# The output projection's low weight parts: negated on ScalarE and completed by an adding transfer

## The chip, the cores and the metric

The kernel runs on one core of one Trainium2 chip. The metric is the device time of one execution in microseconds (us); lower is better. A core has five engines that run side by side and wait for each other through semaphores: TensorE (PE in the rows, its weight loads PEld), VectorE (DVE), ScalarE (ACT), GpSimd (POOL) and SyncE (SP), and 16 DMA engines that carry out the transfers which SP, ACT and POOL issue.

## What is computed

One decoder layer on 256 tokens of width 2048. The reference, cut to what matters here:

```python
proj = jnp.einsum('bsd,de->bse', x, w_in[l])
q_mo, k_mo, v_mo, g_mo, u_gm, v_gm, g_gm, q_me, g_me = jnp.split(proj, IN_SPLIT_POINTS, axis=-1)
...
y_mo = moba_attention(q_mo, k_mo, v_mo).reshape(b, s, MOBA_W) * jax.nn.silu(g_mo)
y_gm = gmlp_spatial_gate(u_gm, v_gm, gmlp_ln_g[l], gmlp_ln_b[l], gmlp_w_s[l], gmlp_b_s[l]) * jax.nn.silu(g_gm)
...
y = jnp.concatenate([y_mo, y_gm, y_me], axis=-1)
sub = jnp.einsum('bse,ed->bsd', y, w_out[l])
x = layer_norm(DEEPNORM_ALPHA * x + sub, ln_g[l], ln_b[l])
```

The change concerns the last product, `y` (256 x 2048) by `w_out` (2048 x 2048), all in float32.

## The kernel before

Every large product is done with operands that are sums of two float32r parts, a high part `hi` and a low part `lo = w - hi`. Three matmuls, hi by hi, hi by lo and lo by hi, stand for one product (`mm3`, lines 105 to 107). So each weight that comes from memory is first split: ScalarE writes `hi` as a converted copy (line 100), VectorE writes `lo` as the raw weight minus `hi` (line 101).

The weights come as one stream of pieces of 128 x 1024 float32 (512 KB). The list STREAM gives their order; the last five items are the column blocks of `w_out`, three of 512 columns (8 pieces each) and two of 256 (4 pieces each): 32 pieces. `load_piece(n)` has a transfer issued on SP's queue into `wraw` (line 146) and the two split instructions. `wraw` has six buffers, `whi` and `wlo` four each (`bufs=LEAD + 1`). While piece n is multiplied, pieces up to n + 3 are asked for:

```python
for m in range(LEAD + 1):
    load_piece(first_piece[i] + j + m)
```

A buffer of `whi` or `wlo` can thus be written again once TensorE is through with the piece four places earlier; a buffer of `wraw` can be loaded again once its last reader is done. The tile framework puts in the waits and sets each engine's order; every engine and every queue works in its own order.

In the output projection a piece of a 512-wide item takes 12 matmuls of 512 columns: two tiles of rows, two halves of the tokens, three products. A piece of a 256-wide item has four tiles of rows and 24 matmuls of 256 columns. In the very last item (`apart=True`) the first half of the tokens goes through all four pieces, then the second half, so that the layer norm of the first half (`finish(0)`, lines 527 to 549, on DVE, ACT and POOL) lies beside the matmuls of the second. `finish(1)` ends the kernel.

Of the kernel before, what the change touches and what calls it, by code (L numbers as in the profile page):

```python
# [13 lines left out]
AF = mybir.ActivationFunctionType  # L14
ALU = mybir.AluOpType
# [16 lines left out]
MAGIC = 1.5 * 2.0 ** 23  # L32
PI_F = 3.1415925

# Column blocks of 128 of w_in: where each part of the projection starts.
Q_MO, K_MO, V_MO, G_MO, U_GM, V_GM, G_GM, Q_ME, G_ME = 0, 8, 16, 24, 32, 36, 40, 44, 48

# The weights' stream. ("T", matrix, block): 128 columns as the stationary operand, which gives the
# projection transposed; ("N", matrix, column, width): columns as the moving operand.
STREAM = [("N", "mem", 4 * P, NW)] + [("T", "mem", b) for b in range(4)]  # L40
STREAM += [("T", "in", Q_ME + b) for b in range(4)] + [("T", "in", G_ME + b) for b in range(4)]
for _g in range(2):
# [2 lines left out]
        STREAM += [("T", "in", K_MO + _h), ("T", "in", Q_MO + _h), ("T", "in", G_MO + _h)]  # L45
STREAM.append(("N", "in", V_GM * P, NW))
STREAM += [("T", "in", U_GM + b) for b in range(4)] + [("T", "in", G_GM + b) for b in range(4)]
# Rows of w_out in the order in which the mixed branches come to be ready.
OUT_ORDER = [0, 1, 2, 3, 4, 5, 6, 7, 12, 13, 14, 15, 8, 9, 10, 11]
OUT_COLS = [(0, 512), (512, 512), (1024, 512), (1536, 256), (1792, 256)]  # L50
STREAM += [("N", "out", c, w) for c, w in OUT_COLS]
# [1 line left out]
PIECE = 1024  # L53
# [2 lines left out]


def pieces_of(item):
    """How many pieces of PIECE elements per partition an item has, and the rows' tiles in each."""
    width = P if item[0] == "T" else item[3]  # L60
    kts = PIECE // width
    return KT // kts, kts, width
# [14 lines left out]
def hymba_layer(ctx: ExitStack, tc: tile.TileContext, xT, memT, x, pos, inv_freq, w, wsT, b_s,  # L77
                gln_g, gln_b, ln_g, ln_b, out):
    nc = tc.nc
# [9 lines left out]
    work = pool("work", 2)  # L89
# [3 lines left out]
    def f32(ap):  # L93
        return ap.bitcast(F32)
# [4 lines left out]
    def split(hi, lo, src):  # L99
        nc.scalar.activation(hi, src, AF.Copy)  # L100
        nc.vector.tensor_tensor(out=lo, in0=src, in1=f32(hi), op=ALU.subtract)  # L101

    def mm3(o, a, b, start, stop):
        """a.T @ b for operands that are exact sums of two float32r parts, (hi, lo)."""
        nc.tensor.matmul(o, a[0], b[0], start=start, stop=False)  # L105
        nc.tensor.matmul(o, a[0], b[1], start=False, stop=False)  # L106
        nc.tensor.matmul(o, a[1], b[0], start=False, stop=stop)  # L107

# [1 line left out]
    zero = const.tile([P, NW], BF16, name="zero")  # L110
    nc.vector.memset(zero, 0.0)
    idle = ps_side.tile([P, NW], F32, tag="side", name="idle")
    for _ in range(N_WARM):
        nc.tensor.matmul(idle, zero[:, :P], zero, start=True, stop=True)

# [1 line left out]
    pieces = []  # L117
    for i, item in enumerate(STREAM):
        n, kts, width = pieces_of(item)
# [8 lines left out]
    def load_piece(n):  # L128
        if n >= len(pieces) or n in ready:
            return  # L130
        i, j, kts, width = pieces[n]
        raw = wp.tile([P, kts, width], F32, tag="wraw", name="wraw", bufs=6)
        hi = wp.tile([P, kts, width], F32R, tag="whi", name="whi", bufs=LEAD + 1)
        lo = wp.tile([P, kts, width], F32R, tag="wlo", name="wlo", bufs=LEAD + 1)
        src = w[n].rearrange("p (k n) -> p k n", k=kts)
        if n == 0:
            a = wp.tile([P, S], F32, tag="araw", name="araw0", bufs=3)
            nc.sync.dma_start(a, memT[:, 0, :])
            for c in range(0, width, S):
                nc.sync.dma_start(raw[:, 0, c:c + S], src[:, 0, c:c + S])  # L140
            first.update(a=a, w=raw[:, 0, :])
            load_act(memT, memX, 1, 1)
            nc.sync.dma_start(raw[:, 1, :], src[:, 1, :])
            split(hi[:, 1, :], lo[:, 1, :], raw[:, 1, :])
        else:
            nc.sync.dma_start(raw, src)
            split(hi, lo, raw)
        if n == 1:
            split(memX[:, 0, 0, :], memX[:, 0, 1, :], first["a"])
        if 0 < n < first_piece[1]:  # L150
            load_act(memT, memX, kts * n, kts)
        ready[n] = (hi, lo)

# [1 line left out]
    memX = big.tile([P, KT, 2, S], F32R, tag="mem", name="memX")  # L155
    xX = big.tile([P, KT, 2, S], F32R, tag="x", name="xX")

# [2 lines left out]
        nc.sync.dma_start(raw[:, :n, :], src[:, k0:k0 + n, :])  # L160
        split(dst[:, k0:k0 + n, 0, :], dst[:, k0:k0 + n, 1, :], raw[:, :n, :])

# [1 line left out]
    slots, clock = {}, [0]  # L164

    def after(n, fn):
# [18 lines left out]
            yield j, kts, ready.pop(first_piece[i] + j)  # L185

    def proj_t(X, hook=None):
        """The next item's projection, transposed: [128 columns, 256 tokens], in SBUF."""
        assert STREAM[item[0]][0] == "T"
        acc = ps_acc.tile([P, 2, S], F32, tag="acc", name="acc")  # L190
        flat = acc.rearrange("p a s -> p (a s)")
        for j, kts, (hi, lo) in next_pieces(hook):
            for m in range(kts):
                k = j * kts + m
                nc.tensor.matmul(flat, hi[:, m, :], X[:, k].rearrange("p a s -> p (a s)"), start=k == 0, stop=False)  # L195
                nc.tensor.matmul(acc[:, 0, :], lo[:, m, :], X[:, k, 0, :], start=False, stop=k == KT - 1)  # L196
                if m % 4 == 3:
                    pump()
        part = work.tile([P, S], F32, tag="part", name="part")
        nc.scalar.activation(part, acc[:, 1, :], AF.Copy)  # L200
        r = work.tile([P, S], F32, tag="projT", name="projT")
        nc.vector.tensor_tensor(out=r, in0=acc[:, 0, :], in1=part, op=ALU.add)  # L202
        return r

    def proj_n(X, order=range(KT), hook=None, apart=False):
        """The next item's projection: two PSUM tiles of [128 tokens, columns]."""
        assert STREAM[item[0]][0] == "N"
        width = STREAM[item[0]][3]
        acc = [ps_acc.tile([P, width], F32, tag="acc", name="acc") for _ in range(NT)]

        def tile_of(t, j, kts, hi, lo):
            for m in range(kts):
                k = order[j * kts + m]
                tk = slice(t * P, (t + 1) * P)
                mm3(acc[t], (X[:, k, 0, tk], X[:, k, 1, tk]), (hi[:, m, :], lo[:, m, :]),
                    j + m == 0, j * kts + m == KT - 1)

        held = []
        for j, kts, (hi, lo) in next_pieces(hook):
            held.append((j, kts, hi, lo))  # L220
            if apart:
                tile_of(0, j, kts, hi, lo)
                continue
            for m in range(kts):
                k = order[j * kts + m]
                if X is memX and k == 0:
                    for c in range(0, width, S):
                        for t in range(NT):
                            nc.tensor.matmul(acc[t][:, c:c + S], first["a"][:, t * P:(t + 1) * P],
                                             first["w"][:, c:c + S], start=c == 0, stop=False)  # L230
                    continue
                for t in range(NT):
                    tk = slice(t * P, (t + 1) * P)
                    mm3(acc[t], (X[:, k, 0, tk], X[:, k, 1, tk]), (hi[:, m, :], lo[:, m, :]),
                        j + m == 0, j * kts + m == KT - 1)
                pump()
        if apart:
            yield acc[0]
            for h in held:
                tile_of(1, *h)  # L240
            yield acc[1]
        else:
            yield from acc

# [1 line left out]
    ident = const.tile([P, P], F32, name="ident")  # L246
    make_identity(nc, ident)
    causal = const.tile([P, 3, P], F32, name="causal")
# [2 lines left out]
        nc.gpsimd.affine_select(out=causal[:, b, :], in_=causal[:, b, :], compare_op=ALU.is_ge, fill=NEG / SCALE,  # L251
                                base=0, pattern=[[-1, P]], channel_multiplier=1)

# [1 line left out]
    cosT = const.tile([P, S], F32, name="cosT")  # L255
    sinT = const.tile([P, S], F32, name="sinT")

# [39 lines left out]
        nc.vector.tensor_scalar(out=sinT[P // 2:], in0=sinT[P // 2:], scalar1=-1.0, scalar2=None, op0=ALU.mult)  # L297

    def split_pair(src, tag, hi=0):
        """src as a tile with its two parts, the high one at index hi."""  # L300
        t = act.tile([P, 2, S], F32R, tag=tag, name=tag, bufs=4)
        split(t[:, hi, :], t[:, 1 - hi, :], src)
        return t
# [30 lines left out]
        nc.gpsimd.tensor_tensor(out=dst, in0=e[:, 0:1], in1=e[:, 1:2], op=ALU.pow)  # L334

    def values(acc, tag):
        """A projection in rows of tokens, as (hi, lo) by tile of tokens."""
        r = []
        for t in range(NT):
            v = act.tile([P, 2, NW], F32R, tag=tag, name=tag, bufs=2)  # L340
            split(v[:, 0, :], v[:, 1, :], acc[t])
            r.append(v)
        return r

# [1 line left out]
    def attention(q, k, v, h, gate, et, is_causal):  # L346
        wide = [P, 2 * P] if is_causal else [2 * P, 2 * P]
        at = [0, wide[0]]
# [68 lines left out]
        after(11, turn)  # L417
        after(14, weigh)

# [1 line left out]
    yX = [None]  # L421

    mv = values(list(proj_n(memX)), "mv")
# [12 lines left out]
        attention(qme[h], mk[h], mv, h, gme, 12 + h, False)  # L436
        gme[h] = silu2(proj_t(xX), "gme", 4)

# [1 line left out]
    late = {}  # L440

    def load_late():
# [23 lines left out]
        if grp == 0:  # L466
            load_late()

# [1 line left out]
    vl = []  # L470
    for acc in proj_n(xX):
        g = gelu2(acc, NW, act.tile([P, NW], F32, tag="vg", name="vg", bufs=2))
# [33 lines left out]
        nc.vector.scalar_tensor_tensor(out=y, in0=um[g], scalar=0.25, in1=gate, op0=ALU.mult, op1=ALU.mult)  # L506
        split(yX[0][:, 8 + g, 0, :], yX[0][:, 8 + g, 1, :], y)

# [1 line left out]
    xs, lg, lb = {}, {}, {}  # L510

    def load_x(n):
# [96 lines left out]
```

## Time and profile before

| | |
|---|---|
| Time of the two runs | 468.15 and 468.91 us, median 468.53 us |
| Span of the profiled execution | 466.4 us (the times count 2.1 us more, median against span) |
| TensorE busy | 449.5 us, 96% |
| VectorE busy | 343.5 us, 74% |
| ScalarE busy | 231.3 us, 50% |
| GpSimd busy | 14.4 us, 3% |
| Output projection's matmuls | from 365 to 453 us of the span |

The span is the time from the first to the last instruction of one profiled execution; no separate time of that execution is given beside it, so 468.53 - 466.4 = 2.1 us is taken for what lies around a span. Busy time is time in which an instruction of the engine was running; an engine can be busy a long time and bound nothing. In the profile L101 is line 101 of the kernel, and `wlo<-wraw,whi` an instruction that reads `wraw` and `whi` and writes `wlo`. A row of the timeline gives start, duration, engine, line, operation and, in brackets, how long the engine sat idle before it and what released it.

### The profile page before, as it was taken

What the parts mean: (1) busy time and instruction counts of PE and PEld (TensorE: products, weight loads), DVE (VectorE), ACT (ScalarE), POOL (GpSimd) and SP (SyncE); (2) the same over time, 40 slices, a digit from 0 to 9 for tenths busy, and PEclk for the clock granted to TensorE, in tenths of its full rate; (3) what the DMA queues carried; (4) which work ended last, traced back from release to release, by engine and by line L of the source; (5) the groups of instructions that cost most, each with busy time, mean ns of one, the idle gap of its engine ahead of it and who ended that gap; (6) DMA issues with size and microseconds to landing.
All of it is one profiled execution on the core that took longest, in us unless ns stands there. A gap on an engine that the chain in (4) does not pass through costs nothing.

```text
span 466.4 us, 6674 instructions
## 1 busy us (share of the span) xinstructions
PE 449.5 (96%) x2465; PEld 386.9 (83%) x2465; DVE 343.5 (74%) x582; ACT 231.3 (50%) x357; POOL 14.4 (3%) x23
## 2 busy tenths in 40 slices
PE   6999999999999999999999999999999999999980
PEld 3888888888888888888888888888888888888980
DVE  3879866776677988885778888858988746465666
ACT  4765754665444555554445545545655543334300
POOL 1000000000000000000000000000200000000033
PEclk9999999999999999999999999999999999999996
DMA  7998776545465555545655455876565557575123
GB/s 268 322 348 275 286 272 225 172 149 161 155 196 179 176 169 182 180 160 163 210 187 180 151 176 200 295 220 204 171 214 181 181 184 237 207 227 184 27 65 135
DMA packets 29552, 91.79 MB, mean 197 GB/s; under 512 B 3408, under 2 KB 5072, under 8 KB 29520
## 3 DMA queue, kind: packets, MB, share of 16 engines
q1 hardware_dynamic: 29232, 90.85, 58.9%
q10 hardware_dynamic: 288, 0.52, 0.3%
q8 instruction: 19, 0.31, 0.3%
q14 instruction: 13, 0.11, 0.1%
HBM read 89.26 MB, written 2.10 MB: 196 GB/s over the span
## 4 chain that ended last, share of the span: by engine, by line
PE 94%; DVE 3%; DMA 1%; SPq 0%; issue 0%; ACT 0%; DVEq 0%
PE acc L195 35%; PE acc L196 18%; PE acc L105 12%; PE acc L106 12%; PE acc L107 12%; DVE hX L544 2%; DMA wraw<-weights 1%; PE ptp L390 1%; DVE hX L545 1%; PE sc L105 1%; PE sc L106 0%; PE sc L107 0%; PE pv L107 0%; PE pv L105 0%; PE pv L106 0%
## 5 line engine op out<-in xcount | busy, mean ns | idle before, releaser
L101 DVE TENSOR_TENSOR wlo<-wraw,whi 128x1024 fp32r<-128x1024 f32 (+1 forms) x152 | 185.5, 1220 | 92.0 <-ACT whi L100 90.7
L100 ACT ACTIVATE whi<-wraw 128x1024 fp32r<-128x1024 f32 (+1 forms) x152 | 160.5, 1056 | 167.6 <-PE acc L195 61.8
L195 PE MATMUL acc<-xX,whi 128*128 128x512 f32 x640 | 227.4, 399 | 0.0
L196 PE MATMUL acc<-xX,wlo 128*128 128x256 f32 x640 | 179.4, 280 | 0.0
L195 PEld LDWEIGHTS acc<-xX,whi 128*128 128x128 f32 x640 | 120.2, 188 | 28.0
L196 PEld LDWEIGHTS acc<-xX,wlo 128*128 128x128 f32 x640 | 120.8, 189 | 0.1
L105 PE MATMUL acc<-whi,yX 128*128 128x512 f32 (+1 forms) x160 | 55.5, 347 | 0.0
L107 PE MATMUL acc<-whi,yX 128*128 128x512 f32 (+1 forms) x160 | 55.5, 347 | 0.0
L106 PE MATMUL acc<-wlo,yX 128*128 128x512 f32 (+1 forms) x160 | 55.5, 347 | 0.0
L105 PE MATMUL acc<-whi,xX 128*128 128x512 f32 x96 | 38.1, 397 | 0.0
L107 PE MATMUL acc<-whi,xX 128*128 128x512 f32 x96 | 37.5, 391 | 0.0
L106 PE MATMUL acc<-wlo,xX 128*128 128x512 f32 x96 | 37.4, 390 | 0.0
L105 PEld LDWEIGHTS acc<-whi,yX 128*128 128x128 f32 x160 | 30.3, 189 | 3.8
L107 PEld LDWEIGHTS acc<-whi,yX 128*128 128x128 f32 x160 | 30.3, 189 | 3.8
L106 PEld LDWEIGHTS acc<-wlo,yX 128*128 128x128 f32 x160 | 30.3, 189 | 3.7
L195 PE MATMUL acc<-memX,whi 128*128 128x512 f32 x64 | 22.6, 399 | 0.0
L107 PEld LDWEIGHTS acc<-whi,xX 128*128 128x128 f32 x96 | 18.0, 188 | 4.0
L105 PEld LDWEIGHTS acc<-whi,xX 128*128 128x128 f32 x96 | 18.0, 188 | 3.4
L106 PEld LDWEIGHTS acc<-wlo,xX 128*128 128x128 f32 x96 | 18.0, 188 | 3.3
L202 DVE TENSOR_TENSOR projT<-acc,part 128x256 f32<-128x256 f32 x44 | 18.1, 413 | 0.0
L196 PE MATMUL acc<-memX,wlo 128*128 128x256 f32 x64 | 18.0, 281 | 0.0
L200 ACT ACTIVATE part<-acc 128x256 f32<-128x256 f32 x44 | 16.1, 369 | 0.0
(147 smaller groups left out, 411.0 us busy)
## 6 DMA issues: line engine op xcount, KB each, us to landing
wraw<-weights SPq DMA_DIRECT2D x151, 512.0 KB, 3.5
araw<-xT SPq DMA_DIRECT2D x8, 256.0 KB, 4.5
araw<-memT SPq DMA_DIRECT2D x7, 256.0 KB, 5.8
xs<-xrow SPq DMA_DIRECT2D x6, 256.0 KB, 4.4
lnp<-ln_gv SPq DMA_DIRECT2D x4, 256.0 KB, 4.5
lnp<-ln_bv SPq DMA_DIRECT2D x4, 256.0 KB, 5.3
out<-hX SPq DMA_DIRECT2D x4, 256.0 KB, 2.6
xs<-xrow SPq DMA_DIRECT2D x4, 128.0 KB, 3.3
```

The source lines that it names most:

```text
L100: nc.scalar.activation(hi, src, AF.Copy)
L101: nc.vector.tensor_tensor(out=lo, in0=src, in1=f32(hi), op=ALU.subtract)
L105: nc.tensor.matmul(o, a[0], b[0], start=start, stop=False)
L106: nc.tensor.matmul(o, a[0], b[1], start=False, stop=False)
L107: nc.tensor.matmul(o, a[1], b[0], start=False, stop=stop)
L195: nc.tensor.matmul(flat, hi[:, m, :], X[:, k].rearrange("p a s -> p (a s)"), start=k == 0, stop=False)
L196: nc.tensor.matmul(acc[:, 0, :], lo[:, m, :], X[:, k, 0, :], start=False, stop=k == KT - 1)
L200: nc.scalar.activation(part, acc[:, 1, :], AF.Copy)
L202: nc.vector.tensor_tensor(out=r, in0=acc[:, 0, :], in1=part, op=ALU.add)
L390: nc.tensor.transpose(tp[:, n, :], st["p"][:, at[t] // P + b, :], ident)
L544: nc.vector.scalar_tensor_tensor(out=o, in0=o, scalar=mvr[:, 0:1], in1=g, op0=ALU.subtract, op1=ALU.mult)
L545: nc.vector.scalar_tensor_tensor(out=o, in0=o, scalar=rs, in1=b, op0=ALU.mult, op1=ALU.add)
```

## The change

For the pieces of `w_out` alone, `lo` is no longer written by VectorE. ScalarE writes `hi` as before and then minus `hi` into `lo`; GpSimd's queue issues a transfer from `wraw` to `lo`, both in SBUF, that adds what it carries to what stands there, `lo = -hi + w`. All other pieces keep their split. The rest of the diff takes comments out.

```diff
         else:
             nc.sync.dma_start(raw, src)
-            split(hi, lo, raw)
+            if STREAM[i][1] == "out":
+                nc.scalar.activation(hi, raw, AF.Copy)
+                nc.scalar.activation(lo, f32(hi), AF.Copy, scale=-1.0)
+                nc.gpsimd.dma_start(f32(lo), raw, accum_op=ALU.add)
+            else:
+                split(hi, lo, raw)
```

Lines move down by five behind this place: L146 is the same in both, L149 is the new activation and L150 the new transfer.

ScalarE at the seam between the last gate projections and the output projection, before (`th`, `part` and `yX` belong to the last mixed branch, the `whi` rows from here on to `w_out`):

```order
L316 ACTIVATE th<-projT 128x256
L100 ACTIVATE whi<-wraw 128x1024
L100 ACTIVATE yX<-ygm 128x256
L100 ACTIVATE whi<-wraw 128x1024 x27
L540 ACTIVATE hX<-hX,nm,ors 128x512
```

The same place after:

```order
L321 ACTIVATE th<-projT 128x256
L148 ACTIVATE whi<-wraw 128x1024
L100 ACTIVATE yX<-ygm 128x256
L149 ACTIVATE wlo<-whi 128x1024
L148 ACTIVATE whi<-wraw 128x1024
L149 ACTIVATE wlo<-whi 128x1024
```

Each `whi` of `w_out` is now followed by a `wlo` of the same size; at the seam a `yX` stands between the two.

GpSimd before, between the two small power instructions of the gMLP's layer norm and the first of `finish(0)`:

```order
L446 AFFINE_SELECT ws<-ws 128x128 x4
L334 TENSOR_TENSOR rs<-rsq 128x1 x2
L334 TENSOR_TENSOR ors<-rsq 128x1
L535 TENSOR_TENSOR nm<-neg,ors 128x1
L541 TENSOR_TENSOR hX<-hX,lnp 128x512
```

And after:

```order
L451 AFFINE_SELECT ws<-ws 128x128 x4
L339 TENSOR_TENSOR rs<-rsq 128x1 x2
L150 DMA wlo<-wraw 128x1024 x32
L339 TENSOR_TENSOR ors<-rsq 128x1
L540 TENSOR_TENSOR nm<-neg,ors 128x1
L546 TENSOR_TENSOR hX<-hX,lnp 128x512
```

The 32 transfers stand in one row on GpSimd, ahead of all its work for the final layer norm.

## Rows read from the trace of the kernel before

**Rows 1.** The page's first part: span; busy time, share and instructions of each engine.

```profile
span 466.4 us, 6674 instructions
PE 449.5 (96%) x2465; PEld 386.9 (83%) x2465; DVE 343.5 (74%) x582; ACT 231.3 (50%) x357; POOL 14.4 (3%) x23
```

**Rows 2.** The page's chain that ended last, by engine, as shares of the span.

```profile
PE 94%; DVE 3%; DMA 1%; SPq 0%; issue 0%; ACT 0%; DVEq 0%
```

**Rows 3.** Stretches: length, busy time (instructions) by engine, TensorE clock, DMA share, GB/s.

```profile
356.00:444.10 88.10, 88.10 (x458) 75.72 (x457) 52.81 (x62) 36.59 (x40) 0.00 (x0) 1.00 0.56 179
444.10:455.30 11.20, 9.19 (x77) 8.99 (x75) 7.66 (x15) 0.82 (x1) 4.03 (x4) 1.00 0.16 54
```

**Rows 4.** Timeline around 400 us: ScalarE's and VectorE's split of one piece.

```profile
400.38 1.06 ACT L100 ACTIVATE whi<-wraw 128x1024 fp32r<-128x1024 f32 x1 [1.66 <-PE acc L107]
...
401.47 1.23 DVE L101 TENSOR_TENSOR wlo<-wraw,whi 128x1024 fp32r<-128x1024 f32 x1 [1.49 <-ACT whi L100]
...
403.10 1.06 ACT L100 ACTIVATE whi<-wraw 128x1024 fp32r<-128x1024 f32 x1 [1.66 <-PE acc L107]
```

**Rows 5.** Instructions on the tile wlo from 356 to 455 us; durations in ns.

```profile
L106 PE MATMUL acc<-wlo,yX x160: 282/389/398, 365.0 to 452.9; 128*128 128x512 f32 x96, 128*128 128x256 f32 x64
L101 DVE TENSOR_TENSOR wlo<-wraw,whi x32: 1204/1226/1226, 357.3 to 442.9; 128x1024 fp32r<-128x1024 f32 x32
```

**Rows 6.** Stretches near the program's start, columns as in Rows 3.

```profile
5.00:10.00 5.00, 3.00 (x11) 1.56 (x10) 1.17 (x3) 2.14 (x4) 0.00 (x0) 1.00 0.92 342
10.00:15.00 5.00, 4.51 (x18) 3.24 (x19) 4.54 (x5) 3.67 (x6) 0.00 (x0) 1.00 0.98 360
```

**Rows 7.** Transfers on wraw, 370 to 445 us: issues, and times from issue to landing.

```profile
L146 SPq DMA_DIRECT2D wraw<-weights x22: 327/328/328, 370.2 to 427.2; - x22
...
DMA to landing us min/median/max: 3.1/4.2/4.6
```

**Rows 8.** What SP's queue waited for, 365 to 430 us: total, times, longest.

```profile
SPq L146 <- DVE wlo L101: 46.0, 21, 2.3
```

**Rows 9.** ScalarE's and VectorE's timeline at the first piece of the output weights.

```profile
356.25 1.05 ACT L100 ACTIVATE whi<-wraw 128x1024 fp32r<-128x1024 f32 x1
357.29 0.42 ACT L100 ACTIVATE yX<-ygm 128x256 fp32r<-128x256 f32 x1
...
357.33 1.23 DVE L101 TENSOR_TENSOR wlo<-wraw,whi 128x1024 fp32r<-128x1024 f32 x1
```

**Rows 10.** Timeline of the end: VectorE, GpSimd and TensorE.

```profile
442.90 1.23 DVE L101 TENSOR_TENSOR wlo<-wraw,whi 128x1024 fp32r<-128x1024 f32 x1
...
447.57 0.42 DVE L562 SCALAR_TENSOR_TENSOR hX<-xs,acc 128x256 f32<-128x256 f32 x1 [3.44 <-PE acc L107]
...
449.12 0.98 POOL L334 TENSOR_TENSOR ors<-rsq 128x1 f32<-128x1 f32 x1 [119.38 <-DVE neg L534]
...
452.77 0.28 PE L105 MATMUL acc<-whi,yX 128*128 128x256 f32 x1
452.89 0.28 PE L106 MATMUL acc<-wlo,yX 128*128 128x256 f32 x1
...
455.23 0.41 DVE L562 SCALAR_TENSOR_TENSOR hX<-xs,acc 128x256 f32<-128x256 f32 x1
```

## The prediction

> **What bounds the kernel now.** I read the page's busy shares first, then the chain of waits, then the stretch that the change touches. TensorE is busy 96% of the span, VectorE 74%, ScalarE 50% [rows 1]; the chain that ended last is TensorE's to 94% and VectorE's to 3% [rows 2]. In the stretch of the output weights, from the first split to the end of the last, TensorE is busy 88.10 of 88.10 us at full clock, while VectorE is busy 52.81 and ScalarE 36.59 [rows 3]. So no split makes TensorE wait there: taking work off VectorE takes away time that nobody waits for.
>
> How much room each step has is read from one piece. ScalarE's `whi` comes 2.72 us after the one before (403.10 - 400.38), each time released by TensorE, which gave a buffer free [rows 4]: 2.72 us is TensorE's pace per 512-wide piece. ScalarE then works 1.06 us and has 1.66 us left, VectorE 1.23 us with 1.49 us idle ahead of it [rows 4]. The DMA engines are busy at a share of 0.56 with 179 GB/s [rows 3]. Early in the program, where loads come without a pause, they move 360 GB/s at a share of 0.98 [rows 6]; I take that for their full rate. A 512 KB piece (524,288 bytes) costs 1.46 us of it.
>
> The end: the last `wlo` is done at 444.13, the first half of the last item's sums reaches VectorE at 447.57, and from there VectorE's row of `finish(0)` and `finish(1)` runs to the end of the span at 466.4; the second half's sums are taken up at 455.23, just behind `finish(0)`, though the last product with `wlo` began at 452.9 [rows 1, 5, 10]. So 447.57 to 466.4, 18.83 us, follows the first half whatever came before.
>
> **The change part by part.**
>
> *VectorE* loses 32 subtractions of 1.226 us [rows 5], 39.2 us. None of it is on the path, since TensorE had no gap in the stretch [rows 3], and the last item's 18.83 us hold no `wlo` (the last one ended 3.4 us before they begin). Worth: 0.
>
> *ScalarE* gains 32 activations. Their price is bounded by the `whi` of the same shape, 1.06 us [rows 4]: 33.9 us in all, 2.12 us of each 2.72. It fits into the 1.66 us that are idle per piece, so it costs 0 as long as pieces go at TensorE's pace; if the pace slackens there is only more room. Behind each new activation waits the next `whi`, which needs a buffer that comes free at the pace of 2.72 us anyway.
>
> *GpSimd* gains 32 issues. The nearest rows are SP's issue of a transfer, 0.33 us [rows 7], and GpSimd's own smallest instruction, 0.98 us [rows 10]. Either is under 2.72 us and GpSimd has nothing else to do in the stretch (busy 0.00, rows 3); I take 0 on the path, and carry the 0.98 into the top of the range. Queued behind the last issue are the power and product instructions of `finish(0)`, which wait for a later result all the same.
>
> *SP's queue*: `wraw` is now given back by the adding transfer and not by VectorE, on whose `wlo` SP waited 46.0 us in 21 waits [rows 8]. A later return holds back only loads that run ahead by six buffers; costed at 0, but it takes away the cover under which loads would run ahead.
>
> *TensorE* waits for the transfer where it waited for VectorE: the first `lo` product of each piece, 32 waits, and all later products queue behind them.
>
> *The DMA engines* gain 32 transfers, the term that decides. The trace has no adding transfer and none from SBUF to SBUF. From below: a piece costs the same as a load, one pass at 360 GB/s, 1.46 us. From above: the transfers go one at a time, each with the median landing of a load, 4.2 us [rows 7], and one more pass for the second operand, 5.66 us, or 6.64 us with GpSimd's 0.98. The operation itself says that two operands are read for each one written (`wraw`, and what stands in `wlo`), so I take two passes, 2.91 us. That is nearest to the saturated stretch [rows 6], since the queue will never be empty.
>
> The Trainium skill, page "Collectives: The Full Stack", section "The bandwidth ceiling: the fold count and why AG ≠ RS ≠ AR", says that a reduction in the DMA engines is slower than a copy because it reads two sources, not because the addition takes cycles, with a ratio of 1.93 measured between HBMs. By it the transfer would be 2.81 us (an estimate) and the time 515 us. No run here shows it yet.
>
> The sum. The first adding transfer can start once ScalarE has written the first `hi` (356.25 + 1.05), the `yX` that stands between (0.42) and `lo` (1.06): 358.8 us [rows 4, 9]. From there the DMA engines must still bring the loads: 179 GB/s over 88.1 us is 15.77 MB [rows 3], less 0.50 MB before 358.8, 15.27 MB, or 42.4 us at 360 GB/s. The adds are 32 x 2.91 = 93.2 us. Together 135.6 us for a stretch of 85: the DMA engines become the bound at some 4.2 us per piece where TensorE needs 2.72. They are through at 494.4. The last one lands 1.64 us later (the shortest landing of a load, 3.1, less its 1.46 [rows 7]), 496.0. TensorE then has the last piece's 12 products of the first half left, 0.12 us apart [rows 10], 1.44 us; then come the 18.83 us of the end. 496.0 + 1.44 + 18.83 = 516.3 us of span, and with the 2.1 us by which the runs' median exceeds the profiled span, 518.4 us: 49.9 us or 10.6% slower.
>
> TensorE will pause in each piece. I cost the pauses at nothing beyond their length: between 5 and 10 us it was busy 3.00 of 5 us and the granted clock stayed 1.00 [rows 6], the upper of its levels, 2.4 GHz.
>
> **The rivals.**
>
> *Hidden, as before (chance 0.20).* If an add costs one pass, the loads and adds are 42.4 + 46.6 = 89.0 us from 358.8, the last lands at 449.4, and the span is 449.4 + 1.44 + 18.83 = 469.7; with 2.1 us, 471.8, 0.7% over. The mechanism is the four `wlo` buffers: a buffer comes back after 1.06 + 1.06 us on ScalarE, the transfer, and 2.72 us of products, and four pieces take TensorE 10.9 us, so a transfer of up to 6.0 us from issue to landing is covered as long as the DMA engines keep up with one every 2.72 us. Loads that land in 4.2 us at a share of 0.56 [rows 3, 7] speak for it; that a load and a one-pass add together already need 2.91 us of DMA per piece speaks against. It decides below about 1.7 us of DMA time per add; up to there the time stays under 478.
>
> For the length of the round trip the Trainium skill, page "DMA: Bandwidth & Descriptors", section "Anatomy of one DMA — SWDGE (gpsimd) path", gives 2.0 us plus the bytes at 436 GB/s for a transfer issued by GpSimd. That would be 3.2 us (an estimate), and this rival's time; it is stated for copies, and no run here shows it.
>
> *One at a time (chance 0.28).* If an adding transfer cannot overlap the next, because each reads, adds and writes back before GpSimd's queue goes on, then 32 x 5.66 = 181.1 us follow 358.8, and the span is 539.9 + 1.44 + 18.83 = 560.2, the time 562. It decides from 4.2 us per transfer, where it passes the DMA engines' sum. Loads on SP's queue do overlap (4.2 us to land at a pace of 2.72), which speaks against. Three passes of 1.46 us (two read, one written, each at the full rate) would give much the same, 565.
>
> *VectorE's relief shows (chance 0.02).* If TensorE waited somewhere for VectorE in this stretch, taking 39.2 us off would make the kernel faster. The most that it could give is TensorE's idle time, 0 of 88.10 us [rows 3]. I know of no place; the chance is for what the trace leaves out.
>
> **How the numbers follow.** The forecast has 0.50: an add between about 1.7 and 4.2 us of DMA time, 479 to 560 us. Hidden 0.20, one at a time 0.28, relief 0.02. A measurement of this kernel can tell about 2%, 9.4 us, from no change. So faster by over 2% has 0.02, within 2% 0.20, slower 0.78. The range goes from 470, just under the one-pass time of 471.8, to 595, the one-at-a-time time with GpSimd's 0.98 us on each transfer (358.8 + 32 x 6.64 + 1.44 + 18.83 + 2.1 = 593.7); I leave out some 0.07 below and 0.10 above.
>
> **What the profile after would show.** If right: TensorE waits at L106 for the transfer of L150, some 1.5 us in each of 32 pieces; the DMA share in the stretch is 0.9 or more; adds land much later than 4.2 us because they queue; VectorE and ScalarE are idle half of the time; up to 358 us and in the last 19 us nothing has changed. A DMA share near 0.6 beside long waits at L106 would mean the transfers go one at a time; TensorE without gaps would mean they are hidden. I would be wrong if an add moves at another rate than two passes, if descriptors made by GpSimd take longer than the 2.72 us of a piece, or if the loads suffer more than their share beside the adds.

## The result, and the profile after

The changed kernel takes 506.15 us (505.65 to 506.66) against 468.53: a ratio of 1.08 with a 95% interval of 1.0767 to 1.0833, 37.6 us slower. The forecast was 518.4.

The page's first part and the chain of waits of the changed kernel, columns as before:

```profile
span 505.0 us, 6773 instructions
...
PE 461.1 (91%) x2465; PEld 389.0 (77%) x2465; DVE 306.0 (61%) x550; ACT 264.2 (52%) x389; POOL 42.4 (8%) x55
...
PE 73%; DMA 16%; issue 5%; DVE 3%; ACT 1%; SPq 0%; POOL 0%; DVEq 0%; POOLq 0%
```

VectorE lost 37.5 us of work and ScalarE gained 33 [rows 1], and neither is where the time is: transfers, which had 1% of the chain, have 16% [rows 2].

The stretch from the first adding transfer to the landing of the last, with the one before it, and two short ones inside it (length, busy time by engine, TensorE's clock, DMA share, GB/s):

```profile
340.00:358.80 18.80, 18.80 (x114) 16.64 (x113) 14.02 (x25) 10.47 (x17) 0.03 (x1) 1.00 0.49 178
358.80:484.50 125.70, 99.11 (x465) 77.27 (x465) 13.74 (x27) 66.69 (x68) 27.96 (x32) 0.97 1.02 255
...
374.00:378.00 4.00, 0.74 (x4) 0.27 (x2) 0.00 (x0) 2.11 (x2) 0.87 (x1) 1.00 1.05 262
378.00:382.00 4.00, 3.48 (x9) 2.70 (x10) 0.00 (x0) 0.00 (x0) 0.00 (x0) 0.60 1.05 234
```

Up to 358.8 us nothing has changed. From there TensorE, which had no gap before [rows 3], is busy 99 of 126 us, VectorE 14 and ScalarE 67. The DMA engines are busy all the time: share 1.02 against 0.56, 255 GB/s against 179. (The share can pass 1, since packets of two queues overlap.) The two short rows show a longer pause of TensorE and what its granted clock did next, which is taken up below.

The instructions on `wlo` (duration in ns, least, median and most; then the first and last start) and the landing times of the adding transfers:

```profile
L149 ACT ACTIVATE wlo<-whi x32: 1043/1060/1062, 357.4 to 477.3; 128x1024 fp32r<-128x1024 f32 x32
L150 POOL DMA_DIRECT2D wlo<-wraw x32: 860/869/1053, 358.8 to 478.6; - x32
...
DMA to landing us min/median/max: 4.7/10.1/12.3
```

The new activation costs 1.06 us, as the `whi` of its shape. An issue on GpSimd costs 0.87 us. An add takes 10.1 us to land in the median, 4.7 at the least. The queues between 365 and 480 us, q0 with the adds and q1 with the loads (packets, MB, the time that packets took as a share of the 16 engines):

```profile
q0 software_dynamic: 4217, 15.32, 68.8%
q1 hardware_dynamic: 4742, 15.07, 34.7%
```

By its packets 512 KB of adds took 0.688 x 115 us x 0.524 / 15.32 = 2.71 us of the 16 engines and 512 KB of loads 1.39 us; the expectations of the experiments go by these two. Who waited, between 355 and 500 us (total, times, longest), and then SP's queue alone:

```profile
POOL wlo L150 <- ACT wlo L149: 107.9, 26, 29.2
DVE hX L567 <- PE acc L107: 103.7, 6, 30.9
ACT whi L148 <- PE acc L107: 38.1, 22, 6.2
PEld acc L106 <- DMA wlo<-wraw: 36.4, 26, 4.2
PE acc L106 <- DMA wlo<-wraw: 26.5, 25, 3.8
...
ACT whi L148 <- DMA wraw<-weights: 12.6, 6, 3.6
```

```profile
SPq L146 <- DMA wlo<-wraw: 93.1, 26, 7.8
```

This is a ring of waits to be read from its members that wait for no engine. TensorE at line 106 waits for the adding transfer, and ScalarE waited six times for a load of weights; the other long waits are for TensorE, or for an engine that waits itself. The chain's 16% on transfers are 12% on the adds and 3% on the loads of weights. SP's loads wait for the same adds, which now give `wraw` back, 93.1 us in place of the 46.0 on VectorE [rows 8].

The end, VectorE's timeline:

```profile
486.14 0.42 DVE L567 SCALAR_TENSOR_TENSOR hX<-xs,acc 128x256 f32<-128x256 f32 x1 [5.96 <-PE acc L107]
...
493.77 0.41 DVE L567 SCALAR_TENSOR_TENSOR hX<-xs,acc 128x256 f32<-128x256 f32 x1
```

From 486.14 to the end of the span it is 18.86 us, against 18.83 [rows 10]. All of the loss lies between 358.8 and 486.

### The profile page after: what moved, and what is told of

Same layout as the page of the kernel before. It is cut to its first block, busy times and chain, and to the rows that moved or that the text cites. A ratio compares the mean times of both kernels' runs of the same rounds, so it can differ in the third digit from the quotient of the medians.

```text
span 505.0 us, 6773 instructions
## 1 busy us (share of the span) xinstructions
PE 461.1 (91%) x2465; PEld 389.0 (77%) x2465; DVE 306.0 (61%) x550; ACT 264.2 (52%) x389; POOL 42.4 (8%) x55
## 4 chain that ended last, share of the span: by engine, by line
PE 73%; DMA 16%; issue 5%; DVE 3%; ACT 1%; SPq 0%; POOL 0%; DVEq 0%; POOLq 0%
PE acc L200 33%; PE acc L201 16%; DMA wlo<-wraw 12%; PE acc L106 7%; PE acc L107 7%; PE acc L105 7%; DMA wraw<-weights 3%; DVE hX L549 1%; PE ptp L395 1%; DVE hX L550 1%; PE sc L105 0%; ACT whi L148 0%; PE sc L106 0%; PE sc L107 0%; PE pv L105 0%
## 5 line engine op out<-in xcount | busy, mean ns | idle before, releaser
L100 ACT ACTIVATE whi<-wraw 128x1024 fp32r<-128x1024 f32 (+1 forms) x120 | 126.6, 1055 | 121.3 <-PE acc L200 59.0
L101 DVE TENSOR_TENSOR wlo<-wraw,whi 128x1024 fp32r<-128x1024 f32 (+1 forms) x120 | 146.4, 1220 | 59.2 <-ACT whi L100 58.1
L106 PE MATMUL acc<-wlo,yX 128*128 128x512 f32 (+1 forms) x160 | 59.5, 373 | 26.6 <-DMA wlo<-wraw 26.5
L567 DVE SCALAR_TENSOR_TENSOR hX<-xs,acc 128x512 f32<-128x512 f32 (+1 forms) x10 | 5.8, 580 | 107.6 <-PE acc L107 103.7
L148 ACT ACTIVATE whi<-wraw 128x1024 fp32r<-128x1024 f32 x32 | 33.8, 1057 | 52.1 <-PE acc L107 38.1
L107 PE MATMUL acc<-whi,yX 128*128 128x512 f32 (+1 forms) x160 | 56.9, 357 | 0.0
L105 PE MATMUL acc<-whi,yX 128*128 128x512 f32 (+1 forms) x160 | 56.7, 356 | 0.0
L150 POOL DMA_DIRECT2D wlo<-wraw x32 | 28.0, 875 | 122.0 <-ACT wlo L149 107.9
L107 PE MATMUL acc<-whi,xX 128*128 128x512 f32 x96 | 37.5, 391 | 0.0
L149 ACT ACTIVATE wlo<-whi 128x1024 fp32r<-128x1024 f32 x32 | 33.9, 1058 | 0.9
L339 POOL TENSOR_TENSOR rs<-rsq 128x1 f32<-128x1 f32 x2 | 3.7, 1859 | 260.2 <-DVE rsq L338 260.2
L107 PEld LDWEIGHTS acc<-whi,xX 128*128 128x128 f32 x96 | 18.0, 188 | 3.9
## 6 DMA issues: line engine op xcount, KB each, us to landing
wlo<-wraw POOLq DMA_DIRECT2D x32, 512.0 KB, 10.1
```

The lines of the kernel that those rows point to most:

```text
L148: nc.scalar.activation(hi, raw, AF.Copy)
L149: nc.scalar.activation(lo, f32(hi), AF.Copy, scale=-1.0)
L150: nc.gpsimd.dma_start(f32(lo), raw, accum_op=ALU.add)
L567: nc.vector.scalar_tensor_tensor(out=hX[:, t, cs], in0=xs[t, n], scalar=ALPHA, in1=acc, op0=ALU.mult, op1=ALU.add)
```

## The experiments

The theory under test is saturation: an add reads two operands, costs the DMA engines two passes, and with the loads beside it they are full. Its rivals: the price is one of each single transfer (a round trip, one at a time, GpSimd's issue), or of the added work on ScalarE. Each edit is shown against the changed kernel; ratios are to the kernel before, which was measured again beside the runs: 469.39 us beside the copy, the adds without loads, every second piece and three buffers, 468.24 beside the two runs of the next section, 468.02 beside the other four.

### ScalarE's part alone, and VectorE's relief alone

```diff
-                nc.gpsimd.dma_start(f32(lo), raw, accum_op=ALU.add)
+                nc.vector.tensor_tensor(out=lo, in0=raw, in1=f32(lo), op=ALU.add)
```

> ScalarE writes minus hi into lo as in the change, but VectorE adds the raw weights onto it instead of the transfer. This is the change's ScalarE part alone. If that part is free, as forecast: 468 to 470 us, with TensorE without a gap in the output projection. If the 34 us of ScalarE or its order at the seam hold something up: 473 or more.

Measured: 468.91 us, ratio 1.0012 (0.9997 to 1.0028).

```diff
-                nc.gpsimd.dma_start(f32(lo), raw, accum_op=ALU.add)
```

> ScalarE writes minus hi into lo and nothing is added, so lo is not the low part and the sums are off; the transfer is left out and VectorE's 32 subtractions too. If VectorE's relief is worth nothing, as forecast: 468 to 470 us. If VectorE held TensorE or the end up somewhere: 466 or less.

Measured: 469.57 us, ratio 1.0011 (0.9994 to 1.0028). A stretch of the output projection in the first and in the second:

```profile
360.00:440.00 80.00, 80.00 (x397) 67.94 (x396) 46.55 (x53) 63.38 (x65) 0.00 (x0) 1.00 0.57 188
```

```profile
360.00:440.00 80.00, 80.00 (x397) 67.98 (x397) 12.23 (x23) 62.74 (x64) 0.00 (x0) 1.00 0.56 187
```

TensorE is busy 80 of 80 us in both, with ScalarE at 63 instead of some 33 of a like stretch, and with VectorE at 47 or at 12. So ScalarE's 34 us cost nothing and VectorE's 39 us bring nothing that these runs could tell (both intervals end at 0.3%), and the loss is the transfer's.

### The same transfer without the addition

```diff
-                nc.gpsimd.dma_start(f32(lo), raw, accum_op=ALU.add)
+                nc.gpsimd.dma_start(f32(lo), raw)
```

> The transfer of line 150 carries the raw piece into lo without adding, so lo is the whole weight and not its low part (the sums come out as nearly twice the product); every instruction, wait and buffer stays, only the second read of the transfer goes. Saturation (the DMA engines are full, and an add costs two passes): one pass of 1.39 us instead of 2.71, so loads and copies need 40.4 + 44.5 = 85 us in a stretch of 85, and the time falls back to 468 to 476 us. If the price is GpSimd's way of issuing, or the added step of negating on ScalarE: 500 to 508. If each transfer's round trip is the price: it shortens by about one pass, 1.4 us, of 10, and the time stays over 490.

Measured: 480.89 us, ratio 1.0238 (1.02 to 1.0276). Two thirds of the loss are gone, though waits and buffers are those of the change and the issue is only a little shorter; but 5 us more stay than the theory allowed. Queues of this kernel between 360 and 440 us (packets, MB, the time that packets took as a share of the 16 engines):

```profile
q1 hardware_dynamic: 4169, 14.04, 51.4%
q0 software_dynamic: 3850, 14.00, 43.7%
```

The copies took 0.437 x 80 = 35.0 us for 14.00 MB, 1.31 us per 512 KB. GpSimd's issue took 0.54 us here, 0.87 in the change.

### The adds without the loads

```diff
-        raw = wp.tile([P, kts, width], F32, tag="wraw", name="wraw", bufs=6)
+        held = STREAM[i][1] == "out" and "out" in first
+        if held:
+            raw = first["out"].rearrange("p k n -> p (k n)").rearrange("p (k n) -> p k n", k=kts)
+        else:
+            raw = wp.tile([P, kts, width], F32, tag="wraw", name="wraw", bufs=6)
...
-            nc.sync.dma_start(raw, src)
+            if not held:
+                nc.sync.dma_start(raw, src)
+            if STREAM[i][1] == "out":
+                first.setdefault("out", raw)
```

> All 32 pieces of the output weights are taken from the first one's buffer, which is loaded once; the loads of the other 31 are left out, so the output projection multiplies by the first piece 32 times. Splits and adding transfers stay. Saturation: the adds alone need 32 x 2.71 = 86.7 us from 358.8, the last lands at about 447, and the time is 468 to 476. If adds go one at a time, at no less than the shortest landing of 4.7 us: 32 x 4.7 = 150 us, over 525. If the loads have nothing to do with it: 506.

Measured: 479.21 us, ratio 1.0218 (1.0194 to 1.0242). The queue of the adds between 360 and 440 us, and the landing times:

```profile
q0 software_dynamic: 3846, 14.05, 92.9%
...
DMA to landing us min/median/max: 4.5/5.7/8.3
```

The adds took 0.929 x 80 = 74.3 us for 14.05 MB, 2.77 us per 512 KB: 2.1 times the copy. They land in 5.7 us, yet run at a pace of 2.72 for long stretches, so two are under way at a time: the rival "one at a time" is out (it asked for over 525). Adds alone nearly fill the DMA engines. Again some 3 us stay beyond the top of the expectation.

### Fewer bytes added: every second piece, every fourth piece, half of each piece

```diff
-            if STREAM[i][1] == "out":
+            if STREAM[i][1] == "out" and j % 2 == 0:
```

> Only every second piece of the output weights is split by the adding transfer; the others are split by VectorE as before. Saturation: 40.4 us of loads and 16 x 2.71 = 43.4 of adds are 84 us in a stretch of 85, so nearly all of the loss goes: 468 to 476. If each transfer costs a wait of its own (round trip, issue, or the order on ScalarE): half of the 37.6 us, about 487.

Measured: 485.61 us, ratio 1.0357 (1.0311 to 1.0404). The theory's 468 to 476 is missed, and the rival's 487 nearly met. A wait per transfer was thus open again; the next two runs test it.

```diff
-            if STREAM[i][1] == "out":
+            if STREAM[i][1] == "out" and j % 4 == 0:
```

> Every fourth piece of the output weights is split by the adding transfer, 8 in all; the others by VectorE. Saturation: 42.4 us of loads and 8 x 2.62 = 21 of adds leave a quarter of the DMA engines' time free, so the loss should go but for a short pause or two: 468 to 472. If each add costs a wait of its own, as the run with every second piece might be read (16 adds, 16 us): 8 us, about 476.

Measured: 470.21 us, ratio 1.0045 (1.003 to 1.0061), 2.2 us slower. A price per transfer would have left 8. The stretch and the landing times of this kernel:

```profile
360.00:440.00 80.00, 80.00 (x398) 67.87 (x397) 37.54 (x44) 39.74 (x42) 6.18 (x8) 1.00 0.83 240
...
DMA to landing us min/median/max: 4.5/4.9/5.5
```

TensorE has no gap. The slowest add lands in 5.5 us, under the 6.0 us that the four buffers cover by the prediction's working. Where the remaining 2.2 us are, its profile (span 466.6, the quickest of its runs) does not show.

```diff
-                nc.scalar.activation(lo, f32(hi), AF.Copy, scale=-1.0)
-                nc.gpsimd.dma_start(f32(lo), raw, accum_op=ALU.add)
+                h = kts // 2
+                nc.scalar.activation(lo[:, :h], f32(hi[:, :h]), AF.Copy, scale=-1.0)
+                nc.gpsimd.dma_start(f32(lo[:, :h]), raw[:, :h], accum_op=ALU.add)
+                nc.vector.tensor_tensor(out=lo[:, h:], in0=raw[:, h:], in1=f32(hi[:, h:]), op=ALU.subtract)
```

> Every piece of the output weights is halved: half of its columns (or rows' tiles) by the adding transfer of 256 KB, half by VectorE. The bytes added are those of the run with every second piece, spread evenly. If what that run lost came from bytes alone (full DMA engines): 483 to 489 again. If it came from the length of the single add beside run-ahead loads, against a buffer that must be ready in time: an add of 256 KB lands some 1.3 us or more sooner and 468 to 475 is expected.

Measured: 479.79 us, ratio 1.0257 (1.0229 to 1.0286). It lies between the two expectations. Over the kernel before, 32 transfers of 256 KB cost 11.8 us and 16 of 512 KB 16.2, so there is no price per transfer; but nearly three quarters of the loss of every second piece stay with the same bytes. Stretch and landing times:

```profile
360.00:440.00 80.00, 73.45 (x316) 58.58 (x315) 27.54 (x47) 44.67 (x57) 22.58 (x26) 0.98 1.00 256
...
DMA to landing us min/median/max: 3.3/5.8/9.3
```

The DMA engines are as full (1.00) as in the changed kernel, and the slowest add takes 9.3 us.

### Do loads that run ahead make the adds late?

```diff
-        raw = wp.tile([P, kts, width], F32, tag="wraw", name="wraw", bufs=6)
+        raw = wp.tile([P, kts, width], F32, tag="wraw", name="wraw", bufs=4)
```

This on top of every second piece.

> As the run with every second piece, but with four buffers of raw weights instead of six in the whole program, so that loads run less far ahead of their use. If adds are late because loads that nobody needs yet share the DMA engines with them: under 480. If the sum of bytes alone counts: 484 to 489. If the shorter run-ahead itself makes loads late: more than that.

Measured: 485.71 us, ratio 1.0385 (1.0322 to 1.0447), the same as with six buffers. That theory of mine falls: with the same bytes the time is the same, however far ahead of use they are loaded.

### Three buffers for the parts instead of four

```diff
-LEAD = 3
+LEAD = 2
```

> The high and low parts have three buffers instead of four, and pieces are asked for two ahead instead of three, in the whole program. Saturation: the adds stay limited by the DMA engines, at about 3.9 us per piece, 506 to 518. If the time from a buffer's return to the landing of its add sets the pace (about 2.3 + 10 + 2.7 us shared by the buffers), a third as much again per piece, 5.0 us instead of 3.9: about 540.

> The kernel before with three buffers instead of four for the high and low parts and pieces asked for two ahead, the control for the same edit in the changed kernel, which measured 522. If the three buffers cost only where adds must land: 468 to 471. If they cost in the whole program: up to 485, and the 16 us are not the adding transfers'.

Measured: 522.06 us (ratio 1.1126, 1.1099 to 1.1154) for the changed kernel with this edit, 472.0 (1.0088, 1.0068 to 1.0108) for the kernel before with it, 4.0 over its own and 1 over the top of what was expected of an edit that costs only where adds must land. So the edit costs 4 us by itself and 12 more where adds must land. With 4 taken off, 518 is the top of what saturation allowed and far from 540. It doesn't decide cleanly: with three buffers only 3 x 2.72 - 2.12 - 2.72 = 3.3 us are covered, less than any add's 4.5, so the buffers' return also counts here.

### What the runs say together

DMA time needed per 512-wide piece is an estimate from the runs: 1.46 us for the load, 1.31 for a copy, 2.77 for an add alone and 2.60 for one beside loads (worked out in the next section). The residual's rows `xs` must be counted too: 512 KB for each eight pieces, 0.18 us a piece. TensorE's pace is 2.72 us. Beside it stand the DMA share and TensorE's waits for a transfer at line 106, each from the one profiled execution:

| kernel | DMA time per piece while loads run | share of 2.72 | DMA share, 360 to 440 us | TensorE's waits | over the kernel before |
|---|---|---|---|---|---|
| the kernel before | 1.46 + 0.18 = 1.64 | 60% | 0.58 | 0 | 0 |
| every fourth piece | 1.46 + 0.18 + 0.65 = 2.29 | 84% | 0.83 | 0 | 2.2 us |
| adds without loads | 0.18 + 2.77 = 2.95 | 108% | 0.98 | 6.9 us | 9.8 us |
| half of each piece | 1.46 + 0.18 + 1.30 = 2.94 | 108% | 1.00 | 7.7 us | 11.8 us |
| copy without addition | 1.46 + 0.18 + 1.31 = 2.95 | 108% | 0.96 | 6.4 us | 11.5 us |
| every second piece | 1.46 + 0.18 + 1.30 = 2.94 | 108% | 0.96 | 12.4 us | 16.2 us |
| the change | 1.46 + 0.18 + 2.60 = 4.24 | 156% | 1.04 | 26.5 us | 37.6 us |

The loss follows the DMA engines' load, and where the sum leaves room the measured share is near it (0.58 and 0.83). I had missed the middle rows because I summed over the whole stretch, where loads and copies just fit (42.4 + 41.9 = 84.3 us in 85.3). While loads run they do not fit, and the time that is free behind the last loads of weights comes too late: from 446 to 450 us the copy's kernel has a share of 0.56. What TensorE loses it cannot win back, since without the transfers it is busy 80 of 80 us. But 0.22 us a piece make at most some 7 us over 32 pieces, and 10 to 16 were lost. In all four kernels of the middle rows the slowest transfer landed later than the 6.0 us that the prediction's working covers, 7.3 to 9.3 us after its issue. In the kernel without loads it can be read what lay beside. The add issued at 383.2 us landed in 5.3 us; the next one, with the residual's rows issued just behind it, in 8.3:

```profile
L157 POOL DMA_DIRECT2D wlo<-wraw x1: 869/869/869, 385.9 to 385.9; - x1
...
DMA to landing us min/median/max: 8.3/8.3/8.3
```

```profile
L528 SPq DMA_DIRECT2D xs<-xrow x2: 328/398/469, 386.2 to 386.9; - x2
```

TensorE then waited 2.4 us, its longest wait there. These rows are not the only cause: with every second piece the longest wait, 3.5 us, was for an add issued at 433.4 that landed in 9.3 us beside two loads of weights and the next add. How the rest of the loss in the middle rows divides is not shown.

## Why the prediction was right

Direction and range held, and the mechanism is the forecast one; the sum of the transfers was too large.

- *VectorE's relief is worth nothing, ScalarE's work costs nothing.* Right, each shown by a run at 1.001.
- *GpSimd's issue, 0 on the path.* Right: 0.87 us, within the 0.33 to 0.98 by which it was bounded, under the pace of a piece.
- *SP's queue, 0 on the path.* Not quite: its waits doubled, ScalarE waited 12.6 us for loads, and these loads have 3% of the chain, where they had 1%. In the sum that is the same full DMA engines and no second price. With fewer buffers of `wraw`, tried with every second piece, nothing got worse.
- *The start at 358.8.* Right: the first issue is at 358.8.
- *Two passes per add, and the DMA engines become the bound.* The price is right in kind: removing the addition left a copy of 1.31 us where the add took 2.77, and the share went to 1.02. That the second half is the second read, and not the addition itself, no run tells apart. The size was off. From 358.8 the last landing was forecast 137.2 us later, at 496.0; the last add was issued at 478.6 and landed 5.8 us later, at 484.4, 125.6 us. Of these 11.6 us, 6.5 lie in the adds, 2.71 us each by their packets instead of 2.91, and 2.0 in the loads, 1.39 instead of 1.46. The other 3.1 are that packets of the two queues overlapped (share above 1), while the sum laid them end to end and put 1.64 us of landing behind. With the loads left at 42.4 us, the 125.7 us of the stretch give an add (125.7 - 42.4) / 32 = 2.60 us, the table's figure. I had priced both passes at the rate of a load from memory, 1.46 us; a pass from SBUF to SBUF took 1.31 in the copy's run, and two of those are 2.62. By time, 12.25 us were missed (518.4 - 506.15); what is beyond the 11.6 are small terms, such as 1.7 us around the span (506.66 against 505.0) where 2.1 were added.
- *1.44 us of the last piece's products, then 18.83 us.* Right: 484.4 to 486.14, 1.7 us, then 18.86.
- *TensorE's pauses cost no more than their length.* Wrong: in the changed kernel TensorE was busy 0.74 of 4 us from 374, and its granted clock in the next 4 us was 0.60. The DMA share was 1.05 in both rows, so the transfers that set the pace went on; that the slower TensorE cost little here is a reading, and no run shows it. In the run with every second piece the price can be read:

```profile
442.73 0.58 PE L106 MATMUL acc<-wlo,yX 128*128 128x256 f32 x1 [3.52 <-DMA wlo<-wraw]
```

```profile
438.00:442.00 4.00, 1.21 (x6) 0.75 (x4) 3.54 (x5) 1.62 (x2) 0.87 (x1) 0.96 1.02 266
442.00:446.00 4.00, 3.27 (x15) 3.27 (x16) 0.14 (x1) 0.00 (x0) 0.00 (x0) 0.50 0.78 232
446.00:450.00 4.00, 4.00 (x26) 4.00 (x26) 0.00 (x0) 1.92 (x2) 0.00 (x0) 0.68 0.04 15
450.00:454.00 4.00, 4.00 (x35) 4.00 (x35) 1.23 (x1) 1.25 (x2) 0.87 (x1) 1.00 0.60 115
```

After a wait of 3.5 us for an add the clock is 0.50, the lower level of 1.2 GHz, then 0.68, then full. Where 35 products go through in 4 us at full clock, 15 and 26 do. That is some 29 products of 0.12 us, 3.5 us (an estimate, with 0.7 us of the wait in it), and the same profile has a second such fall from 462 to 470. No run isolated the clock. The copy's kernel shows a loss without it: its clock stayed at 1.00 from 360 to 440 us.

The rivals: *hidden* would have needed an add under 1.7 us; the copy at 1.31 shows that even there 11.5 us are lost, so the point from which that rival decides was set too high (and by the prediction's own sum 478 is reached at 1.65 us, not 1.7). *One at a time* fell with the adds that overlap at a pace of 2.72. *VectorE's relief* fell with the run that leaves the addition out.

The Trainium skill, page "Collectives: The Full Stack", section "The bandwidth ceiling: the fold count and why AG ≠ RS ≠ AR", gives two source reads as the reason why a reduction is slower than a copy and 1.93 as the measured ratio of an AllGather's bandwidth to a ReduceScatter's. This case is near it: 2.77 to 1.31 us of packet time, 2.1, within SBUF; the reason itself no run here shows. By the Trainium skill, page "DMA: Bandwidth & Descriptors", section "Anatomy of one DMA — SWDGE (gpsimd) path", a transfer of 512 KB issued by GpSimd takes 3.2 us (an estimate). This case agrees for the first copy, which met no load and landed in 3.1 us, and for the shortest, 2.9; in the stream beside loads the median was 5.8:

```profile
L150 POOL DMA_DIRECT2D wlo<-wraw x32: 540/540/757, 358.3 to 451.0; - x32
...
DMA to landing us min/median/max: 2.9/5.8/7.3
```

## What to carry to other kernels

Work moved from an engine that nobody waits for to the DMA engines is not free: add up the DMA time per step of the bounding engine, loads included, count an adding transfer as two copies, leave out no small load, and compare it with the step while loads run, not only over the whole stretch. At 84% of the step the adds were nearly free (2.2 us), at 108% they cost 10 to 16 us, and at 156% the DMA engines set the pace (37.6 us). Before freeing an engine, look whether anyone waits for it in that stretch.

## What was not expected of the hardware

- By its packets an adding transfer of 512 KB within SBUF took 2.71 us of the 16 engines' time beside loads and 2.77 without them, a copy 1.31; a load from memory took 1.39 beside the adds. GpSimd's issue took 0.87 us for the add and 0.54 for the copy.
- After a wait of 3.5 us TensorE's granted clock was 0.50 in the 4 us that followed, while between 5 and 10 us of the kernel before it was busy 3.00 of 5 us and the clock stayed at 1.00 [rows 6].
- Where the DMA engines were asked for 108% of the bounding engine's pace while loads ran, 10 to 16 us were lost over 32 pieces, although the excess itself is at most some 7.
